# Seven block products in one more k-pair of the down projection, and wider additions for their activation sums

## The chip, the core and the metric

One core of a Trainium2 chip runs the whole program. TensorE (PE in the profile, PEld for its weight loads) multiplies, VectorE (DVE), ScalarE (ACT) and GpSimd (POOL) work beside it, and SyncE (SP) issues most of the DMAs. The metric is the device time of one launch in microseconds. Lower is better.

## The reference

One decoder layer on 256 tokens of width 2048, in float32:

```python
x = x + 0.5 * swiglu(rms_norm(x, g1), w_gate, w_up, w_down)        # FFN 1, hidden width 5632
h = rms_norm(x, gm); z = h @ w_in
x = x + concat(gated_linear_attention(z), dilated_attention(z)) @ w_out
x = x + 0.5 * swiglu(rms_norm(x, g2), w_gate2, w_up2, w_down2)     # FFN 2
# swiglu(x, g, u, d) = (silu(x @ g) * (x @ u)) @ d
```

The change is in the last product of `swiglu`, the down projection (256 x 5632 by 5632 x 2048), of both FFNs.

## The kernel before

**Splitting.** Every float32 operand is held as a rounded high part and the rest, its low part (`wh`, `wl` of weights; `hh`, `hl` and `uh`, `ul` of activations). A product is three matmuls into one PSUM bank: high by high, high by low, low by high. `split` makes the two parts: ACT copies with rounding (L113), then DVE subtracts (L114).

**The down projection.** It runs over two column pairs (`cp` 0 and 1) of 1024 output columns each, so there are four of them in the program. Each goes over the 44 blocks of 128 of the hidden width, taken two at a time as 22 k-pairs. A k-pair's weights, 256 x 1024, come by one DMA of 1 MB into a `raw` tile, of which there are three (L219, SP's queue). The order of the k-pairs of a column pair is written out by hand in `DOWN_ORDERS`: "s" for a k-pair done plainly, "g" for one done by seven products.

- A plain k-pair (`products`, L276 to L280) is two units of 128 of the hidden width; each has two token tiles, two banks and three matmuls. That makes 24 matmuls of 512 columns, and two weight splits of 1024 elements per partition on ACT and DVE.
- A k-pair by seven products (`seven_products`, L301 to L303) treats tokens, hidden and output columns as 2 x 2 blocks and needs 7 block products, so 21 matmuls. It needs sums of weight blocks: `prepare` makes four jobs of it, "plain" (a sum into the room `urs`, L240, and a split), "last" (a split of 512), "sums" (a split of the room, and two additions into `raw`, L248) and "more" (a split of what these additions left in `raw`). It also needs four sums of activation blocks, split as well: `seven_forms` makes them once for an FFN, and both column pairs use them.

The four extra accumulators of the seven products are added to the output after the last "g" of a column pair: `fold`, nine operations, one in each following step.

**What sets the order.** `weights()` prepares jobs two ahead of the unit in hand; weight tiles come from a ring of four (`WBUF`). Other work sits in the list `later`, from which a few entries are taken in each step (a unit has two steps, one for each token tile). For the down projection `later` has 32 entries: a call of `seven_forms` in every fifth, and the rest of the gate and up stage's work in the others. From this program order a planner, which runs a time line of its own, draws up the final order of each engine's queue; each queue is then worked in that order.

**Where sums are kept.** The split sums (`dforms`) live in parts of `hh` and `hl`, which the down projection does not need otherwise. `hl` 8 to 11 is the room of the "last" job. After the first column pair of FFN 1 (`renorm`, `norm_moved`) POOL moves blocks of the new activations into `hh` 8 to 15, so these parts serve no form from then on, except that those into 12 to 15 wait until form 0 has been used.

Of the kernel before, what the change touches and what calls it, by code (L numbers as in the profile page):

```python
# [14 lines left out]
F32 = mybir.dt.float32  # L15
# [3 lines left out]
ALU = mybir.AluOpType  # L19
AX = mybir.AxisListType  # L20

P = 128
S = 256
# [15 lines left out]
def _order(text):  # L39

    seven, plain = iter(range(text.count("g"))), iter(range(text.count("g"), len(text)))
    return [(next(seven), True) if c == "g" else (next(plain), False) for c in text]


FF_ORDERS = [_order("ssgssgss" if b in FF_SEVEN else "ssssssss") for b in range(FF // 512)]
DOWN_ORDERS = [_order("ssssssgssgssgsgsgsgsss"), _order("sgsssgssgssgssgsgsssss")]


def layer_kernel(tc, x, xT, gains, gla_gate_up, gla_gate_bias, gla_out_norm, att_q_norm, att_k_norm,
                 w_ff1, w_dn1, w_mix, w_low, w_out, w_ff2, w_dn2, c_sq, c_rope, c_mask, out):  # L50

    nc = tc.nc
# [3 lines left out]
    with ExitStack() as es:  # L56
# [20 lines left out]
        def t512(name):  # L77
            return cst.tile([P, 512], F32, name=name, tag="t512", bufs=4)
# [14 lines left out]
        hh = cst.tile([P, KT, S], F32R, name="hh")  # L93
# [81 lines left out]
        def jobs_of(w, orders):  # L175
            for cp, order in enumerate(orders):
                for kp, seven in order:
                    for part in ("plain", "last", "sums", "more") if seven else (0, 1):
                        yield w, cp * len(order) + kp, part

        jobs = [*jobs_of(w_ff1, FF_ORDERS), *jobs_of(w_dn1, DOWN_ORDERS)]
        jobs += [(w_mix, i, k) for i in range(3 * KT // 2) for k in range(2)] + ["low"]
        jobs += [(w_mix, i, k) for i in range(3 * KT // 2, 3 * KT) for k in range(2)]
        jobs += [(w_out, i, k) for i in range(w_out.shape[0]) for k in range(2)]
        jobs += [*jobs_of(w_ff2, FF_ORDERS), *jobs_of(w_dn2, DOWN_ORDERS)]

        AHEAD = 2
        ready = []
# [74 lines left out]
        def alt(a):  # L263

            return a.rearrange("p (b a) -> p a b", b=2)
# [24 lines left out]
        def seven_products(cs, ms, acts, forms, first, last):  # L290

            tok = [slice(t * P, (t + 1) * P) for t in range(NT)]
            a11, a12, a22 = [[a[:, acts[k][2], tok[t]] for a in acts[k][:2]] for t, k in ((0, 0), (0, 1), (1, 1))]
            s1, s3, s2, sa = [[f[:, i, :] for f in forms] for i in range(4)]

            def product(bank, a, ws, j, start, stop):  # L300
                nc.tensor.matmul(bank, lhsT=a[0], rhs=alt(ws[0][:, j, :]), start=start, stop=False)  # L301
                nc.tensor.matmul(bank, lhsT=a[0], rhs=alt(ws[1][:, j, :]), start=False, stop=False)  # L302
                nc.tensor.matmul(bank, lhsT=a[1], rhs=alt(ws[0][:, j, :]), start=False, stop=stop)  # L303

            ws = weights()
            product(ms[0], a11, ws, 0, first, last)
            product(cs[0], sa, ws, 1, False, False)
            product(cs[1], a12, weights(), 0, False, False)
            ws = weights()
            product(ms[1], s1, ws, 0, first, last)  # L310
            product(ms[3], s3, ws, 1, first, last)
            ws = weights()
            product(ms[2], s2, ws, 0, first, last)
            product(cs[3], a22, ws, 1, False, False)

        def seven_forms(acts, forms, full, sums):

            for k, (ah, al, i) in enumerate(acts):
                nc.vector.tensor_add(full[:, k * S:(k + 1) * S], ah[:, i, :].bitcast(F32), al[:, i, :].bitcast(F32))
            a11, a21, a12, a22 = [full[:, i * P:(i + 1) * P] for i in range(4)]  # L320
            sums = sums.rearrange("p (i q) -> p i q", i=4)
            nc.vector.tensor_sub(sums[:, 0, :], a22, a21)
            nc.vector.tensor_sub(sums[:, 1, :], a11, a21)
            nc.vector.scalar_tensor_tensor(sums[:, 2, :], sums[:, 0, :], -1.0, a11, op0=ALU.mult, op1=ALU.subtract)
            nc.vector.tensor_add(sums[:, 3, :], a12, sums[:, 2, :])
            split(*forms, sums)

# [81 lines left out]
        def ffn(name, done, residual, extra=None, final=False):  # L409

            with tc.tile_pool(name=name, bufs=1, reuse_waits="tile") as fp:
# [12 lines left out]
                for b in range(FF // 512):  # L424
# [23 lines left out]
                    if b == FF_SEVEN[0]:  # L448
# [8 lines left out]
                        forms = {kp: [f[:, kp] for f in fs] for kp in range(2)}  # L457
# [22 lines left out]
                dacts = [part(k) for k in range(FT)]  # L480

                def lent(a, k, i):
                    return a[:, k:k + 2, :].rearrange("p k (t q) -> p (k t) q", q=P) if i else a[:, k:k + 2, :].rearrange("p k s -> p (k s)").unsqueeze(1)

                rooms["down"] = {"sum": urs, "wh": lent(hl, 8, 0), "wl": lent(hl, 10, 0)}
                dforms = {kp + 1: [lent(hh, 2 * kp, 1), lent(hl, 2 * kp, 1)] for kp in range(4)}
                dforms[0] = [lent(hh, 12, 1), lent(hh, 14, 1)]
                dforms[5] = [lent(hl, 12, 1), lent(hl, 14, 1)]
                rest, later[:] = later[:], []
                for step in range(32):  # L490
                    kp = step // 5 - 1
                    if step % 5 == 0 and 0 <= kp < 6:
                        later.append(lambda kp=kp: seven_forms(dacts[2 * kp:2 * kp + 2], dforms[kp], t512("full"), t512("sums")))
                    else:
                        later.append(rest.pop(0) if rest else lambda: None)
                for cp in range(2):
                    def evac(t, ps, cp=cp):
                        for j in range(2):
                            c = 2 * cp + j
                            blk = xs[:, t, c * 512:(c + 1) * 512]  # L500
                            nc.vector.scalar_tensor_tensor(halves(blk), ps[j], 0.5, halves(blk), op0=ALU.mult, op1=ALU.add)
                            done(t, c, blk)

                    def fold(m, cp=cp):
                        a, b = [halves(urs[:, i, :]) for i in range(2)]
                        c = [[halves(xs[:, t, i * 512:(i + 1) * 512]) for i in (2 * cp, 2 * cp + 1)] for t in range(NT)]

                        def add(c, a, f):
                            return lambda: nc.vector.scalar_tensor_tensor(c, a, f, c, op0=ALU.mult, op1=ALU.add)
                        return [lambda: nc.scalar.activation(a, m[0], AF.Copy),  # L510
                                lambda: nc.vector.tensor_add(b, a, m[2]), add(c[0][1], a, 0.5),
                                lambda: nc.vector.tensor_add(a, b, m[3]), add(c[1][1], a, 0.5),
                                lambda: nc.vector.tensor_add(b, b, m[1]), add(c[0][0], b, -0.5),
                                lambda: nc.vector.tensor_add(a, a, m[1]), add(c[1][0], a, -0.5)]

                    holding[0] = NT - cp
                    seven_pair(dacts, DOWN_ORDERS[cp], dforms, cp, evac, fold, span=28 if cp else 32, final=final and cp == 1)
                spare.close()


# [444 lines left out]
```

## Time and profile before

| | us |
|---|---|
| median of 3 runs | 1721.78 |
| lowest and highest of them | 1718.25, 1723.28 |
| profiled execution, its own time | 1721.82 |
| its span, first to last instruction | 1720.0 |

| engine | busy us | share of the span |
|---|---|---|
| PE | 1707.9 | 99% |
| PEld | 1486.0 | 86% |
| DVE | 1399.7 | 81% |
| ACT | 936.0 | 54% |
| POOL | 506.4 | 29% |

The granted TensorE clock is 1.000 throughout. A matmul's record is longer than the distance to the next one, since matmuls are pipelined; the distance between starts is what a matmul costs. Rows of DVE overlap by about 0.08 us in the same way. The four column pairs of the down projection lie at about 455 to 565 and 565 to 677 us (FFN 1), and 1495 to 1606 and 1606 to 1716 us (FFN 2).

### The profile page before, as it was taken

To read this page: it belongs to the slowest core of one execution; us is meant where nothing else is said; L and a number is where in the kernel's file an instruction comes from. 1 tells how busy PE (TensorE), PEld (TensorE's weight loads), DVE (VectorE), ACT (ScalarE), POOL (GpSimd) and SP (SyncE) were. 2 spreads that over 40 slices of the span, in tenths; PEclk is the share of its full clock that TensorE was granted. 3 is DMA by queue.
4 is the path that set the end of the run, shared out by engine and by line. 5 is a ranking of instruction groups with operands and counts; after the bars stand their busy time and mean duration, and the time that the engine had idled before them with its cause. 6 is when DMAs were issued, how large, how long until landed. Compare 5 with 4: busy or idle time off the path is not lost.

```text
span 1720.0 us, 22310 instructions
## 1 busy us (share of the span) xinstructions
PE 1707.9 (99%) x7980; PEld 1486.0 (86%) x7980; DVE 1399.7 (81%) x1699; ACT 936.0 (54%) x1166; POOL 506.4 (29%) x1002
## 2 busy tenths in 40 slices
PE   9999999999999999999999999999999999999999
PEld 7888888888888888888888888888888888888887
DVE  6888888888899788578865667798988888898876
ACT  7555555555555555564654545555555555465453
POOL 0333333444410611054250043333333334420000
PEclk9999999999999999999999999999999999999999
DMA  8666655655675657576564466666666656665754
GB/s 344 212 228 224 216 208 213 228 211 211 239 269 220 217 208 245 185 243 231 195 205 171 149 216 236 219 221 229 228 227 227 214 208 221 222 246 215 249 205 147
DMA packets 85807, 378.62 MB, mean 220 GB/s; under 512 B 21392, under 2 KB 38800, under 8 KB 42688
## 3 DMA queue, kind: packets, MB, share of 16 engines
q1 hardware_dynamic: 50864, 350.25, 56.6%
q0 software_dynamic: 34112, 25.88, 5.3%
q8 instruction: 62, 1.02, 0.2%
q10 hardware_dynamic: 720, 1.07, 0.2%
q14 instruction: 49, 0.40, 0.1%
HBM read 354.57 MB, written 4.19 MB: 209 GB/s over the span
## 4 chain that ended last, share of the span: by engine, by line
PE 76%; DVE 11%; DMA 7%; issue 3%; ACT 2%; POOL 1%; DVEq 0%; ACTq 0%; SPq 0%; POOLq 0%
PE acc L278 18%; PE acc L280 18%; PE acc L276 18%; DVE wl L114 5%; DMA raw<-in_w_ff_dram 4%; PE tp L280 3%; PE tp L278 3%; PE tp L276 3%; PE acc L302 3%; PE acc L303 3%; PE acc L301 3%; DVE raw L248 1%; ACT wh L113 1%; DVE xs L240 1%; DMA hh<-us 1%
## 5 line engine op out<-in xcount | busy, mean ns | idle before, releaser
L113 ACT ACTIVATE wh<-raw 128x1024 fp32r<-128x1024 f32 (+1 forms) x660 | 676.0, 1047 | 476.2 <-PE acc L280 188.3
L114 DVE TENSOR_TENSOR wl<-raw,wh 128x1024 fp32r<-128x1024 f32 (+1 forms) x658 | 787.7, 1215 | 169.1 <-ACT wh L113 165.8
L135 POOL DMA_DIRECT2D xs<-us x704 | 344.4, 497 | 556.4 <-issue 353.1
L280 PE MATMUL acc<-wh,hl 128*128 128x512 f32 x1232 | 371.0, 380 | 0.0
L278 PE MATMUL acc<-wl,hh 128*128 128x512 f32 x1232 | 370.5, 380 | 0.4 <-DVE wl L114 0.3
L276 PE MATMUL acc<-wh,hh 128*128 128x512 f32 x1232 | 363.0, 381 | 2.6 <-ACT wh L113 2.6
L276 PEld LDWEIGHTS acc<-wh,hh 128*128 128x128 f32 x1232 | 232.6, 189 | 37.0 <-ACT wh L113 3.3
L278 PEld LDWEIGHTS acc<-wl,hh 128*128 128x128 f32 x1232 | 232.5, 189 | 34.5 <-DVE wl L114 1.3
L280 PEld LDWEIGHTS acc<-wh,hl 128*128 128x128 f32 x1232 | 232.6, 189 | 32.8
L278 PE MATMUL acc<-wl,uh 128*128 128x512 f32 x384 | 116.7, 379 | 0.0
L280 PE MATMUL acc<-wh,ul 128*128 128x512 f32 x384 | 116.6, 379 | 0.0
L276 PE MATMUL acc<-wh,uh 128*128 128x512 f32 x384 | 111.9, 379 | 0.2 <-ACT wh L113 0.2
L135 POOL DMA_DIRECT2D hh<-us x128 | 62.0, 499 | 124.0 <-DVE us L128 67.6
L276 PEld LDWEIGHTS acc<-wh,uh 128*128 128x128 f32 x384 | 72.5, 189 | 10.9 <-ACT wh L113 0.6
L280 PEld LDWEIGHTS acc<-wh,ul 128*128 128x128 f32 x384 | 72.6, 189 | 10.3
L278 PEld LDWEIGHTS acc<-wl,uh 128*128 128x128 f32 x384 | 72.6, 189 | 10.3
L240 DVE TENSOR_TENSOR xs<-raw 128x1024 f32<-128x1024 f32 x40 | 48.2, 1206 | 37.3 <-DMA raw<-in_w_ff_dram 37.3
L113 ACT ACTIVATE wh<-xs 128x1024 fp32r<-128x1024 f32 x40 | 42.1, 1053 | 57.3 <-DVE xs L240 42.0
L276 PE MATMUL tp<-wh,hh 128*128 128x512 f32 x240 | 73.2, 379 | 0.0
L113 ACT ACTIVATE swh<-raw 128x512 fp32r<-128x512 f32 x40 | 25.2, 630 | 88.0 <-DMA raw<-in_w_ff_dram 88.0
L278 PE MATMUL tp<-wl,hh 128*128 128x512 f32 x240 | 71.4, 379 | 0.0
L280 PE MATMUL tp<-wh,hl 128*128 128x512 f32 x240 | 71.4, 379 | 0.0
(284 smaller groups left out, 2358.9 us busy)
## 6 DMA issues: line engine op xcount, KB each, us to landing
raw<-in_w_ff_dram SPq DMA_DIRECT2D x175, 1024.0 KB, 5.1
raw<-in_w_dn_dram SPq DMA_DIRECT2D x88, 1024.0 KB, 4.9
raw<-in_w_mix_dram SPq DMA_DIRECT2D x48, 1024.0 KB, 4.9
raw<-in_w_out_dram SPq DMA_DIRECT2D x16, 1024.0 KB, 4.8
xs<-us POOLq DMA_DIRECT2D x704, 16.0 KB, 3.7
xs<-in_x_dram SPq DMA_DIRECT2D x2, 1024.0 KB, 10.6
xs<-in_x_dram POOLq DMA_DIRECT2D x2, 1024.0 KB, 5.5
hh<-us POOLq DMA_DIRECT2D x128, 16.0 KB, 3.7
```

Source lines behind the costliest of these rows:

```text
L113: nc.scalar.activation(dst_h, src, AF.Copy)
L114: nc.vector.tensor_sub(dst_l, src, dst_h.bitcast(F32))
L135: nc.gpsimd.dma_start(dst[32 * q:32 * q + 32, ..., r * n:(r + 1) * n], src[32 * r:32 * r + 32, ..., q * n:(q + 1) * n])
L240: nc.vector.tensor_add(room["sum"], b1, mid)
L248: nc.vector.tensor_add(raw[:, 1, j, :], b, raw[:, 1, j, :])
L276: nc.tensor.matmul(ps[j], lhsT=sh, rhs=alt(wh[:, j, :]), start=first and i == 0, stop=False)
L278: nc.tensor.matmul(ps[j], lhsT=sh, rhs=alt(wl[:, j, :]), start=False, stop=False)
L280: nc.tensor.matmul(ps[j], lhsT=sl, rhs=alt(wh[:, j, :]), start=False, stop=last and i == len(ws) - 1)
L301: nc.tensor.matmul(bank, lhsT=a[0], rhs=alt(ws[0][:, j, :]), start=start, stop=False)
L302: nc.tensor.matmul(bank, lhsT=a[0], rhs=alt(ws[1][:, j, :]), start=False, stop=False)
L303: nc.tensor.matmul(bank, lhsT=a[1], rhs=alt(ws[0][:, j, :]), start=False, stop=stop)
```

## The change

Three of the four column pairs get a seventh "g": both of FFN 2 (`LAST_ORDERS`) and the first of FFN 1. The second of FFN 1 keeps its six. The new sums of activations lie in `hh` 8 to 11. Seven calls of `seven_forms` now stand in every fourth entry of `later`. In `seven_forms`, two additions of 256 elements become one of 512, and two subtractions of 128 become one of 256; for this the sums s1 and s3 change places in their tile. The first "g" of a first column pair comes after five plain k-pairs instead of six.

```diff
-DOWN_ORDERS = [_order("ssssssgssgssgsgsgsgsss"), _order("sgsssgssgssgssgsgsssss")]
+DOWN_ORDERS = [_order("sssssgssgsgsgsgsgsgsss"), _order("sgsssgssgssgssgsgsssss")]
+LAST_ORDERS = [DOWN_ORDERS[0], _order("sgssgssgssgssgsgsgssss")]
...
-        jobs += [*jobs_of(w_ff2, FF_ORDERS), *jobs_of(w_dn2, DOWN_ORDERS)]
+        jobs += [*jobs_of(w_ff2, FF_ORDERS), *jobs_of(w_dn2, LAST_ORDERS)]
...
-            s1, s3, s2, sa = [[f[:, i, :] for f in forms] for i in range(4)]
+            s3, s1, s2, sa = [[f[:, i, :] for f in forms] for i in range(4)]
...
-            for k, (ah, al, i) in enumerate(acts):
-                nc.vector.tensor_add(full[:, k * S:(k + 1) * S], ah[:, i, :].bitcast(F32), al[:, i, :].bitcast(F32))
+            ah, al, i = acts[0]
+            nc.vector.tensor_add(full.rearrange("p (k s) -> p k s", k=2), ah[:, i:i + 2, :].bitcast(F32), al[:, i:i + 2, :].bitcast(F32))
             a11, a21, a12, a22 = [full[:, i * P:(i + 1) * P] for i in range(4)]
             sums = sums.rearrange("p (i q) -> p i q", i=4)
-            nc.vector.tensor_sub(sums[:, 0, :], a22, a21)
-            nc.vector.tensor_sub(sums[:, 1, :], a11, a21)
-            nc.vector.scalar_tensor_tensor(sums[:, 2, :], sums[:, 0, :], -1.0, a11, op0=ALU.mult, op1=ALU.subtract)
+            nc.vector.tensor_sub(sums[:, 0:2, :], full.rearrange("p (i q) -> p i q", i=4)[:, 0::3, :], a21.unsqueeze(1).to_broadcast([P, 2, P]))
+            nc.vector.scalar_tensor_tensor(sums[:, 2, :], sums[:, 1, :], -1.0, a11, op0=ALU.mult, op1=ALU.subtract)
             nc.vector.tensor_add(sums[:, 3, :], a12, sums[:, 2, :])
             split(*forms, sums)
...
                 dforms[5] = [lent(hl, 12, 1), lent(hl, 14, 1)]
+                dforms[6] = [lent(hh, 8, 1), lent(hh, 10, 1)]
...
-                    kp = step // 5 - 1
-                    if step % 5 == 0 and 0 <= kp < 6:
+                    kp = step // 4 - 1
+                    if step % 4 == 0 and 0 <= kp < 7:
...
-                    seven_pair(dacts, DOWN_ORDERS[cp], dforms, cp, evac, fold, span=28 if cp else 32, final=final and cp == 1)
+                    seven_pair(dacts, (LAST_ORDERS if final else DOWN_ORDERS)[cp], dforms, cp, evac, fold, span=28 if cp else 32, final=final and cp == 1)
```

## Prediction

> **What bounds the kernel now.** I read the page first, then what TensorE waited for, then the busy time of each engine in the four column pairs of the down projection, and last the time lines of one run of "g" k-pairs. The page's engine line and the waits of PE:
>
> ```profile
> PE 1707.9 (99%) x7980; PEld 1486.0 (86%) x7980; DVE 1399.7 (81%) x1699; ACT 936.0 (54%) x1166; POOL 506.4 (29%) x1002
> PE acc L276 <- ACT wh L113: 2.7, 3, 1.9
> PE tp L301 <- ACT wh L113: 1.4, 3, 0.7
> PE tp L302 <- DVE wl L114: 0.5, 1, 0.5
> ```
>
> TensorE is the bound. It hardly waits, and where it does after the start it waits for a weight split. So each matmul that goes takes its distance to the next with it, as long as the splits keep up. That distance and the time of one "g" with one "s" stand in the chain of waits (start, duration, engine and line):
>
> ```profile
> 520.89 0.86 PE acc L276 x4
> 530.60 0.86 PE acc L276 x4
> 540.31 0.86 PE acc L276 x4
> 550.02 0.86 PE acc L276 x4
> ```
>
> These are the first matmuls of the "s" between successive "g". They are 9.71 us apart, and 21 + 24 = 45 matmuls lie between, so one takes 0.2158 us. PE ran there without a pause.
>
> Do the splits keep up? Busy time in the four column pairs:
>
> ```profile
> 455.10:565.40 110.30, 110.30 (x512) 96.58 (x511) 101.66 (x137) 61.69 (x70) 16.74 (x34) 1.00 0.64 234
> 565.40:676.60 111.20, 110.58 (x511) 96.18 (x510) 88.80 (x97) 59.37 (x70) 35.36 (x72) 1.00 0.66 226
> 1495.30:1605.70 110.40, 110.40 (x513) 96.50 (x512) 101.42 (x137) 60.86 (x68) 16.74 (x34) 1.00 0.64 234
> 1605.70:1715.90 110.20, 110.20 (x511) 96.19 (x509) 81.71 (x84) 52.52 (x53) 0.00 (x0) 1.00 0.55 195
> ```
>
> The columns are the stretch and its length, then PE, PEld, DVE, ACT, POOL, clock, DMA share and rate. In the two first column pairs DVE is busy 92% of the time, since the forms of an FFN are made there; in the last it has 28 us to spare.
>
> **The change part by part.**
>
> *Matmuls.* Three k-pairs go from 24 to 21: 9 x 0.2158 = 1.94 us less on PE, all of it on the path. The Trainium skill, TensorE: Matmul & The Clock Gate, section "Back-to-back issue gap", gives about 131 ns for one matmul of 512 columns in a sustained stream. By that the gain would be an estimated 1.18 us and the sum 0.76 us higher; the rows above show 0.2158, so the rule doesn't hold here.
>
> *Sums of activations.* Distances between DVE starts, in FFN 2:
>
> ```profile
> 1526.53 0.28 DVE L322 TENSOR_TENSOR sums<-full 128x128 f32<-128x128 f32 x1
> 1526.73 0.28 DVE L323 TENSOR_TENSOR sums<-full 128x128 f32<-128x128 f32 x1
> 1526.94 0.68 DVE L114 TENSOR_TENSOR hl<-sums,hh 128x512 fp32r<-128x512 f32 x1
> 1527.54 0.28 DVE L324 SCALAR_TENSOR_TENSOR sums<-sums,full 128x128 f32<-128x128 f32 x1
> 1527.74 0.75 DVE L319 TENSOR_TENSOR full<-uh,ul 128x256 f32<-128x256 f32 x2
> 1528.41 1.21 DVE L114 TENSOR_TENSOR wl<-raw,wh 128x1024 fp32r<-128x1024 f32 x1
> 1529.55 0.28 DVE L325 TENSOR_TENSOR sums<-full,sums 128x128 f32<-128x128 f32 x1
> ```
>
> An operation of 128 elements takes 0.20 us, of 256 0.33 (two of them 0.67), of 512 0.60, of 1024 1.14. Two of 256 as one of 512 save 0.07, two of 128 as one of 256 another 0.07. A call falls from 2.07 to 1.93 us of DVE, and the 16 calls there are save 2.2 us. Those in the gate and up stages (4) I take at nothing: they are 0.56 us spread over two stages. Their bounds are 0 and -0.56.
>
> *The added "g" on DVE.* A "g" needs 1.14 (sum) + 1.14 + 0.60 + 1.14 + 1.14 (four splits) + 2 x 0.60 = 6.36 us, an "s" 2 x 1.14 = 2.28. In a first column pair DVE gets 4.08 + 1.93 (form 6) - 6 x 0.14 = 5.2 us more: 101.7 becomes 106.9, of the 109.6 that PE then needs. In the last one 81.7 becomes 85.8. ACT gets three splits of 1024, one of 512 and a form's split for two of 1024, about 2.4 us on 62 of 110: covered. The DMAs stay as they are, one `raw` of 1 MB for a k-pair, and neither POOL nor SP gets another instruction.
>
> *The last column pair of FFN 2.* The gain there is whole. The last "g" comes one k-pair (5.2 us) later, and `fold` with it. In the trace DVE's additions of the fold are past before these rows, and DVE idles until the last outputs:
>
> ```profile
> 1706.69 1.22 DVE L114 TENSOR_TENSOR wl<-raw,wh 128x1024 fp32r<-128x1024 f32 x1 [1.36 <-ACT wh L113]
> 1712.51 1.29 DVE L501 SCALAR_TENSOR_TENSOR xs<-acc,xs 128x512 f32<-128x512 f32 x2 [4.59 <-PE acc L280]
> ```
>
> The split before it too has 1.36 us of idle time ahead of it. A unit takes PE 12 x 0.2158 = 2.59 us, and one split and two additions of 512 take DVE 1.14 + 2 x 0.60 = 2.34, so the fold keeps pace over the last four k-pairs. Cost 0; the 4.59 us are the cover that would have to go first.
>
> *What moves in the queues.* In `later` the load of `xs` (L478, POOL) comes one entry later, after form 2 now. In FFN 1 it was issued at 499.55 and first used by the fold at 548.51, so one entry costs nothing; the cover is 49 us:
>
> ```profile
> 499.55 0.54 POOL L478 DMA_DIRECT2D xs<-in_x_dram  x1 [19.71 <-DVE ul L114]
> 548.51 0.68 DVE L509 SCALAR_TENSOR_TENSOR xs<-urs,xs 128x512 f32<-128x512 f32 x1
> ```
>
> POOL's moves into `hh` 8 to 11 begin in FFN 1 after the first column pair's outputs, three "s" after form 6 was last read: no new wait.
>
> *The first column pairs.* Here the price is open. Two things happen. First, the run of alternating "g" and "s" grows: before, "g" stand at places 9, 12, 14, 16, 18 (counted from 0) and three times a "g" follows two places on; now at 8, 10, 12, 14, 16, 18, five times. What such a run costs DVE, in FFN 1 and then FFN 2 (`urs<-raw` is a "g"'s first sum, and the first of three merged L114 behind it is the "more" split of the "g" before):
>
> ```profile
> 515.59 1.23 DVE L240 TENSOR_TENSOR urs<-raw 128x1024 f32<-128x1024 f32 x1 [0.67 <-DMA raw<-in_w_dn_dram]
> 526.64 1.23 DVE L240 TENSOR_TENSOR urs<-raw 128x1024 f32<-128x1024 f32 x1 [2.07 <-DMA raw<-in_w_dn_dram]
> 527.78 3.49 DVE L114 TENSOR_TENSOR wl<-raw,wh 128x1024 fp32r<-128x1024 f32 x3
> 536.19 1.23 DVE L240 TENSOR_TENSOR urs<-raw 128x1024 f32<-128x1024 f32 x1 [0.72 <-DMA raw<-in_w_dn_dram]
> ...
> 1556.06 1.23 DVE L240 TENSOR_TENSOR urs<-raw 128x1024 f32<-128x1024 f32 x1 [1.10 <-DMA raw<-in_w_dn_dram]
> 1566.74 1.22 DVE L240 TENSOR_TENSOR urs<-raw 128x1024 f32<-128x1024 f32 x1 [1.84 <-DMA raw<-in_w_dn_dram]
> 1577.05 1.23 DVE L240 TENSOR_TENSOR urs<-raw 128x1024 f32<-128x1024 f32 x1 [1.48 <-DMA raw<-in_w_dn_dram]
> 1578.19 3.49 DVE L114 TENSOR_TENSOR wl<-raw,wh 128x1024 fp32r<-128x1024 f32 x3
> ```
>
> The next "g"'s sum stands ahead of this "g"'s "more" split in DVE's queue, and it waits for its DMA. The DMA goes out only when the "s" between has been split, since there are three `raw` tiles, and right behind another:
>
> ```profile
> 517.97 0.33 SPq L219 DMA_DIRECT2D raw<-in_w_dn_dram  x1
> 520.24 0.33 SPq L219 DMA_DIRECT2D raw<-in_w_dn_dram  x1
> ```
>
> From 520.24 to the sum at 526.64 are 6.4 us; the sum, "more" and the two splits of the next "s" then take 1.14 + 3.49 before the next DMA of that kind can go. So the loop turns in 11.05, 9.55, 10.68 and 10.31 us (distances of the sums), against PE's 9.71. It eats up the lead of the splits. In FFN 2 the lead is gone at the end of the run: the "more" split that starts at 1578.19 ends some 0.06 us before its first matmul, which has to wait 0.10 us (0.32 to the next instead of 0.22):
>
> ```profile
> 1579.47 0.48 PE L302 MATMUL tp<-wl,hh 128*128 128x512 f32 x1
> 1579.79 0.38 PE L303 MATMUL tp<-wh,hl 128*128 128x512 f32 x1
> ```
>
> The longer run has four loops with a "g"'s sum ahead; the fifth is the run's end, where no "g" follows and "more" isn't held up. I take the first as the first ones were (11.05 and 10.68, so 1.16 over PE's 9.71) and three as the second ones (9.55 and 10.31, 0.22 over): 1.82 us. The lead on entry, at the second "g", is:
>
> ```profile
> 503.52 2.36 DVE L114 TENSOR_TENSOR wl<-raw,wh 128x1024 fp32r<-128x1024 f32 x2 [1.20 <-ACT wh L113]
> 505.62 0.38 PE L302 MATMUL tp<-wl,hh 128*128 128x512 f32 x1
> ...
> 1543.53 2.36 DVE L114 TENSOR_TENSOR wl<-raw,wh 128x1024 fp32r<-128x1024 f32 x2 [1.20 <-ACT wh L113]
> 1545.79 0.38 PE L302 MATMUL tp<-wl,hh 128*128 128x512 f32 x1
> ```
>
> The first of the two merged splits ends some 1.22 us after its start, 0.88 and 1.04 us ahead of PE, 0.96 in the mean. That leaves 1.82 - 0.96 = 0.9 us of waiting for a column pair. Bounds: 0 (all loops at 9.55) and 4 x 1.34 - 0.96 = 4.4 (all at 11.05).
>
> Second, the first "g" comes one "s" earlier: 24 x 0.2158 = 5.18 us less of PE's time, 2.28 + 0.84 = 3.1 us less of DVE's work to that point, so the lead at the second "g" falls by 2.1, from 0.96 to -1.1. But four of the six forms that stand ahead of it in the program serve only later "g", and their 4 x 1.93 = 7.7 us can move into the loop's waits of 0.7 to 2.1 us. Bounds 0 and 1.2 (0.88 - 2.06); I take 0.3, nearer the end at which the forms yield, since their small operations already stand between the splits in the rows of 1526 to 1529.
>
> *Sum.* 1721.82 (the profiled time, within 0.04 of the median) - 1.94 - 0.10 (the wait at 1579.47, contained in the new 0.9) + 2 x (0.9 + 0.3) = 1722.2 us.
>
> **Rivals.** *All of it is hidden.* DVE has 110.3 - 101.7 = 8.6 us idle in the first column pairs, more than the 5.2 us to be added; if forms and splits fill the waits, no matmul waits longer: 1721.82 - 1.94 - 0.10 = 1719.8. Against it: part of that idle time is waiting for DMAs behind which a queue worked in order stands still.
>
> *The run of "g" is DMA bound (slower).* If each loop takes as long as the longest shown, 11.05 us, and the forms don't yield, a first column pair loses 4.4 + 1.2 = 5.6 us: 1721.82 - 2.04 + 11.2 = 1731.0. It decides above 7.2 us of waits in both together, 3.6 each, (3.6 + 0.96) / 4 = 1.14 over PE's pace, so from a loop of 10.85 us on. For it: two of four loops are at or near that. Against it: the second loops of both runs were shorter. The Trainium skill, DMA: Bandwidth & Descriptors, section "Bandwidth", gives 6.15 us for a DMA of 1 MB. By that a loop would be an estimated 6.15 + 4.6 = 10.8 us, and the time about 1727; the page's row of the profile has a lower median, with single cases near the rule's:
>
> ```profile
> raw<-in_w_dn_dram SPq DMA_DIRECT2D x88, 1024.0 KB, 4.9
> ```
>
> *The planner arranges other stages anew.* The waits of PE listed first (4.6 us together) could shrink to nothing or double with any edit: 1721.82 - 4.6 = 1717 to 1726.
>
> **How the numbers follow.** About 0.3% (5.2 us) is what a measurement of this kernel can tell from no change. Chances: the forecast, partly eaten up, 0.52 (its own range 1720.5 to 1725); all hidden 0.27; DMA bound 0.16; other stages 0.05. The range 1718.5 to 1727.5 reaches from somewhat under the all-hidden case to the middle of the DMA-bound one. Slower by over 0.3% (above 1727.0) takes most of the DMA-bound case and some of the last, 0.13; faster (below 1716.6) needs more than all gains named, 0.04; the rest, 0.83, is within.
>
> **What would show it.** PE with 9 matmuls fewer, at the same distance. Waits of PE for "more" splits at the "g" of places 8 to 16 of both first column pairs, 1.2 us in each; sums `urs<-raw` there 9.6 to 11 us apart, each ended by its DMA. No wait in the last column pair, and DVE's idle time before the last outputs still over 1 us. L319 at 128x512, about 0.68 us each, 18 of them. The prediction is wrong if PE shows no new wait (forms filled the gaps), if it waits at the first "g" already for several microseconds, or if the difference lies in the gate and up or attention stages.

## The result and the profile after

The changed kernel takes 1734.0 us, median of 6 runs (1730.77 to 1737.02), against 1720.55 of before (6 runs): 1.0075 times the time, 95% interval 1.0062 to 1.0088. It is slower by 13 us; 1722.2 was forecast, with a range of 1718.5 to 1727.5. The profiled execution took 1737.02 us itself, the longest of its six runs, with a span of 1735.2.

The page's engine line, and then what PE waited for in the first three column pairs, in order, leaving out waits of up to 0.2 us each (us in total, times, longest):

```profile
PE 1713.1 (99%) x7971; PEld 1483.4 (85%) x7971; DVE 1414.5 (82%) x1692; ACT 938.7 (54%) x1174; POOL 507.8 (29%) x1002
```

```profile
PE tp L303 <- DVE wl L115: 2.1, 3, 1.2
PE tp L302 <- ACT wh L114: 1.4, 1, 1.4
...
PE acc L303 <- DVE wl L115: 1.5, 1, 1.5
PE acc L302 <- ACT wh L114: 0.5, 1, 0.5
...
PE tp L303 <- DVE wl L115: 1.9, 3, 1.2
PE tp L302 <- ACT wh L114: 1.4, 1, 1.4
```

In the fourth pair PE waits for nothing. (Lines of the code are one higher than before.) The two first column pairs with the busy time of each engine, columns as in the prediction:

```profile
456.50:573.30 116.80, 112.66 (x510) 94.96 (x509) 106.04 (x134) 61.96 (x71) 16.77 (x34) 1.00 0.61 218
1505.60:1621.80 116.20, 112.38 (x510) 95.08 (x509) 106.75 (x134) 61.68 (x72) 16.78 (x34) 1.00 0.61 220
```

A first column pair now has 7 x 21 + 15 x 24 = 507 matmuls, 109.4 us at 0.2157; it takes 116.8 and 116.2. So nine matmuls went, as the engine line says, and 7 us of pauses came into each first pair.

To place them, the distance between each matmul of 512 columns and the next was taken wherever it is over 0.235 us, and 0.2157 taken off. These pauses of PE, in us, with the median time of 4 to 12 runs and its ratio to runs of before on the same chip (whose medians were 1720.48 to 1721.9). In those with an asterisk some matmuls behind a pause ran at half pace, 0.427 us each, as the last section shows; they make 0.8 to 1.7 us of the number, in `x4_pool` up to 3:

| kernel | FFN 1, pair 1 | FFN 1, pair 2 | FFN 2, pair 1 | FFN 2, pair 2 | us | ratio, 95% |
|---|---|---|---|---|---|---|
| before | 0.0 | 1.2 | 0.1 | 0.0 | 1720.55 | 1 |
| after | 7.2 | 3.1 | 6.5 | 0.0 | 1734.0 | 1.0075, 1.0062 to 1.0088 |
| x1_wide | 0.2 | 1.7 | 0.0 | 0.0 | 1724.47 | 1.0013, 1.0003 to 1.0023 |
| x2_last | 0.0 | 4.6* | 0.6 | 0.0 | 1724.06 | 1.0017, 1.0007 to 1.0028 |
| x12_lastnarrow | 0.1 | 1.5 | 3.5 | 0.0 | 1721.7 | 0.9995, 0.9985 to 1.0006 |
| x10_narrow7 | 8.0* | 1.6 | 6.7 | 0.0 | 1734.3 | 1.0068, 1.0052 to 1.0084 |
| x18_oneloop | 0.4 | 2.2 | 1.6 | 0.0 | 1725.03 | 1.0020, 1.0009 to 1.0032 |
| x15_shift | 2.4 | 2.9 | 1.9 | 0.0 | 1726.41 | 1.0030, 1.0019 to 1.0040 |
| x11_sixearly | 5.0 | 4.7* | 4.2 | 0.0 | 1731.66 | 1.0053, 1.0038 to 1.0068 |
| x8_sixfirst | 6.8* | 5.6* | 7.0* | 0.0 | 1734.82 | 1.0068, 1.0054 to 1.0082 |
| x16_breaklate | 6.2* | 4.9* | 5.6 | 0.0 | 1733.64 | 1.0074, 1.0057 to 1.0090 |
| x3_pinforms | 7.6* | 2.9 | 6.4* | 0.0 | 1730.66 | 1.0048, 1.0034 to 1.0062 |
| x5_pinsum | 6.1* | 2.2 | 6.1* | 0.0 | 1731.66 | 1.0056, 1.0042 to 1.0069 |
| x6_pinboth | 11.2* | 2.2 | 11.2* | 0.0 | 1740.53 | 1.0116, 1.0103 to 1.0130 |
| x7_before_pinsum | 1.2 | 2.2 | 1.1 | 0.0 | 1722.76 | 1.0013, 1.0004 to 1.0022 |
| x9_oneform | 1.5 | 6.6* | 3.9 | 0.0 | 1731.3 | 1.0062, 1.0048 to 1.0075 |
| x4_pool | 17.1* | 15.2* | 17.3* | 0.0 | 1763.77 | 1.0251, 1.0237 to 1.0265 |

The pauses are those of one profiled execution each, the times medians. How far one execution can stand off another is seen in `x1_wide` and `x2_last`: up to 1534 us their order on DVE is the same, and FFN 1's second pair still has 1.7 us of pauses in the one and 4.6 in the other. From before to after the two spans differ by 15.2 us: -1.9 for the matmuls, +7.2, +2.0 and +6.4 for the first three pairs, and +1.5 in the first 22 us of the program, which the change doesn't touch; the gate and up and attention stages differ by under 0.5 each.

**What a first pair's pauses are.** DVE around the second "g" (place 8) of FFN 1, and PE there:

```profile
498.36 0.68 DVE L249 TENSOR_TENSOR raw<-urs,raw 128x512 f32<-128x512 f32 x1
498.96 0.41 DVE L323 TENSOR_TENSOR sums<-full 128x256 f32<-128x256 f32 x1
499.30 0.68 DVE L320 TENSOR_TENSOR full<-uh,ul 128x512 f32<-128x512 f32 x1
499.90 0.68 DVE L115 TENSOR_TENSOR hl<-sums,hh 128x512 fp32r<-128x512 f32 x1
500.50 0.68 DVE L115 TENSOR_TENSOR ul<-xs,uh 128x512 fp32r<-128x512 f32 x1
501.11 0.68 DVE L249 TENSOR_TENSOR raw<-raw 128x512 f32<-128x512 f32 x1
...
501.16 0.38 PE L304 MATMUL tp<-wh,hl 128*128 128x512 f32 x1
502.93 0.48 PE L302 MATMUL tp<-wh,hh 128*128 128x512 f32 x1 [1.39 <-ACT wh L114]
```

Between the two additions that "more" needs, the planner (the "scheduler" of the expectations) has put a subtraction, an addition and a split of forms, and a split of the FFN's tail: 2.15 us. The three forms are those of the sixth, seventh and fifth "g", which PE begins at 543, 553 and 532 us only. ACT can round the "more" blocks only after the second addition, and PE stands 1.56 us at 501.16 and 3.1 us in all around place 8. DVE has no free moment then; the windows show it (DVE's is the third busy time, behind PE's and PEld's):

```profile
475.00:490.00 15.00, 14.89 (x68) 12.40 (x68) 14.90 (x22) 9.18 (x12) 4.48 (x9) 1.00 0.66 239
490.00:505.00 15.00, 13.15 (x59) 10.55 (x57) 15.00 (x23) 7.89 (x11) 0.54 (x1) 1.00 0.60 211
505.00:520.00 15.00, 14.50 (x64) 11.80 (x65) 14.96 (x19) 8.38 (x10) 0.00 (x0) 1.00 0.64 236
520.00:535.00 15.00, 14.53 (x68) 12.41 (x67) 10.38 (x12) 7.59 (x8) 0.00 (x0) 1.00 0.56 209
```

DVE is full for 45 us and then has 4.6 us idle in the next 15. From place 14 on DVE stands idle for the DMA of each "g"'s sum, as the prediction said. Here are the sums of places 5, 10, 12, 14, 16 and 18, and behind those of 10 to 16 the row that begins with the "more" split of the "g" before:

```profile
474.91 1.23 DVE L241 TENSOR_TENSOR urs<-raw 128x1024 f32<-128x1024 f32 x1 [1.35 <-DMA raw<-in_w_dn_dram]
...
501.71 1.21 DVE L241 TENSOR_TENSOR urs<-raw 128x1024 f32<-128x1024 f32 x1
503.98 1.21 DVE L115 TENSOR_TENSOR wl<-raw,wh 128x1024 fp32r<-128x1024 f32 x1
512.79 1.22 DVE L241 TENSOR_TENSOR urs<-raw 128x1024 f32<-128x1024 f32 x1
514.53 4.62 DVE L115 TENSOR_TENSOR wl<-raw,wh 128x1024 fp32r<-128x1024 f32 x4
524.01 1.23 DVE L241 TENSOR_TENSOR urs<-raw 128x1024 f32<-128x1024 f32 x1 [2.40 <-DMA raw<-in_w_dn_dram]
525.15 2.35 DVE L115 TENSOR_TENSOR wl<-raw,wh 128x1024 fp32r<-128x1024 f32 x2
535.17 1.23 DVE L241 TENSOR_TENSOR urs<-raw 128x1024 f32<-128x1024 f32 x1 [2.32 <-DMA raw<-in_w_dn_dram]
536.31 2.35 DVE L115 TENSOR_TENSOR wl<-raw,wh 128x1024 fp32r<-128x1024 f32 x2
545.24 1.23 DVE L241 TENSOR_TENSOR urs<-raw 128x1024 f32<-128x1024 f32 x1 [1.25 <-DMA raw<-in_w_dn_dram]
```

From sum to sum the loops turn in 11.08, 11.22, 11.16 and 10.07 us; the first is no wait for a DMA, since DVE works through it without a pause. What PE needs is "more", and from "more" to "more" the turns are 10.55, 10.62, 11.16 and 10.07 (to 546.38), together 3.6 us over four of PE's 9.71. PE's pauses behind place 8 are 3.6 us too (FFN 2: 3.3 and 3.4): nothing of the loops is hidden any more.

### The profile page after: what moved, and what is told of

The parts are those of the page before. It is cut to its first block, busy times and chain, and to the rows that moved or that the text cites. A ratio compares the mean times of both kernels' runs of the same rounds, so it can differ in the third digit from the quotient of the medians.

```text
span 1735.2 us, 22294 instructions
## 1 busy us (share of the span) xinstructions
PE 1713.1 (99%) x7971; PEld 1483.4 (85%) x7971; DVE 1414.5 (82%) x1692; ACT 938.7 (54%) x1174; POOL 507.8 (29%) x1002
## 4 chain that ended last, share of the span: by engine, by line
PE 72%; DVE 14%; DMA 7%; issue 3%; ACT 2%; POOL 1%; DVEq 0%; ACTq 0%; SPq 0%
PE acc L279 16%; PE acc L281 16%; PE acc L277 16%; DVE wl L115 7%; PE tp L277 4%; PE tp L281 4%; PE tp L279 4%; PE acc L303 3%; PE acc L304 3%; DMA raw<-in_w_ff_dram 3%; PE acc L302 3%; DMA raw<-in_w_dn_dram 2%; DMA xs<-us 2%; ACT wh L114 1%; DVE raw L249 1%
## 5 line engine op out<-in xcount | busy, mean ns | idle before, releaser
L279 PE MATMUL acc<-wl,uh 128*128 128x512 f32 x364 | 111.5, 381 | 0.1
L281 PE MATMUL acc<-wh,ul 128*128 128x512 f32 x364 | 110.9, 379 | 0.0
L277 PE MATMUL acc<-wh,uh 128*128 128x512 f32 x364 | 106.7, 381 | 1.3 <-ACT wh L114 1.2
L277 PEld LDWEIGHTS acc<-wh,uh 128*128 128x128 f32 x364 | 68.2, 189 | 13.3 <-ACT wh L114 3.9
L279 PEld LDWEIGHTS acc<-wl,uh 128*128 128x128 f32 x364 | 68.1, 189 | 11.7 <-DVE wl L115 2.3
L281 PEld LDWEIGHTS acc<-wh,ul 128*128 128x128 f32 x364 | 68.8, 189 | 9.8
```

The lines of the kernel that those rows point to most:

```text
L277: nc.tensor.matmul(ps[j], lhsT=sh, rhs=alt(wh[:, j, :]), start=first and i == 0, stop=False)
L279: nc.tensor.matmul(ps[j], lhsT=sh, rhs=alt(wl[:, j, :]), start=False, stop=False)
L281: nc.tensor.matmul(ps[j], lhsT=sl, rhs=alt(wh[:, j, :]), start=False, stop=last and i == len(ws) - 1)
```

## The experiments

Theory A: PE comes to the second "g" before DVE has done what stands ahead of its "more" split. Theory B: the loops with a "g"'s sum ahead are slower than PE, each by its own excess. Rivals: C, the wider operations let the planner set another order elsewhere; D, DVE is simply full.

**Wide operations alone, and the last pair alone.** `x1_wide` is before with the new `seven_forms`; `x2_last` adds `LAST_ORDERS` for FFN 2's second pair; `x12_lastnarrow` is that with the old `seven_forms`; `x10_narrow7` is after with the old `seven_forms`.

```diff
-                    if step % 5 == 0 and 0 <= kp < 6:          # x2_last, x12_lastnarrow, against before
+                    if final and step == 31:
+                        kp = 6
+                    if (step % 5 == 0 and 0 <= kp < 6) or kp == 6:
```

> The kernel before with only the wider operations of seven_forms; every column pair keeps its six 'g'. Theory A (backlog: too much of DVE's work stands ahead of the first 'more' splits of the longer run) and theory B (loop: in an alternating run the next 'g''s sum waits for its DMA ahead of 'more') both say that the 13 us come from the seventh 'g' alone: 1720.6 us, at most 0.5 less, and no wait at the 'g' of the first column pairs. Rival C (the wider operations let the scheduler set another order, which holds up splits elsewhere, as in FFN 1's second column pair, 2 us more after): several microseconds slower, 1723 to 1730.

> The kernel before with the wider operations, and the seventh 'g' in FFN 2's second column pair alone. A and B: that pair has no alternating run and DVE has 28 us idle there, so three matmuls go at no cost: 0.65 us below the kernel with the wider operations alone, about 1719.9 us, PE without waits in that pair. C: like the wider operations alone or slower, 1723 to 1730.

> The kernel before with one change: the seventh 'g' in FFN 2's second column pair, with the operations of seven_forms as before and the seventh form made at the end of the list. Three matmuls less on PE with DVE 28 us idle there: 0.65 us below before, 1719.9; no waits in that pair. The added form of 2.1 us in FFN 2's first column pair could cost up to as much: 1722. If the list's other order moves FFN 1's stages: up to 1724.

> The kernel after with the narrower operations of before in seven_forms, all else as after: DVE gets 0.14 us more for each form. If the seventh 'g' makes the loss, 1734 to 1736 us. If the wider operations make part of it by the order that the scheduler sets (rival C; alone they came out at 1.0013 of before), up to 2 us less, 1731 to 1733.

The wide operations alone put no pause into the first pairs: the seventh "g" and its order make the loss there. By time, `x1_wide` is slower than before by 0.13%, some 2 us, where A and B had expected none, so C has a part. `x2_last` against `x12_lastnarrow`, another pair with wide and narrow operations, differs by 0.22%; after against `x10_narrow7` by 0.07%, less than their intervals, though the latter's first pair has 1.4 us at half pace. So the size of this part isn't settled. The seventh "g" in the last pair costs nothing in that pair, in any kernel that has it. The 0.65 us that it saves are less than the runs can tell; `x2_last` and `x12_lastnarrow` came out above the 1719.9 expected. The 3.5 us of `x12_lastnarrow` in FFN 2's first pair are mostly one pause of 2.7, for a "more" behind a sum that waited 3.64 us for a DMA which took 7.7 us to land.

What C is in FFN 1's second pair can be seen. First after, then `x10_narrow7`: DVE, and SP's issue of the next "g"'s weights:

```profile
631.72 2.35 DVE L115 TENSOR_TENSOR wl<-raw,wh 128x1024 fp32r<-128x1024 f32 x2
...
636.77 1.23 DVE L241 TENSOR_TENSOR urs<-raw 128x1024 f32<-128x1024 f32 x1 [2.70 <-DMA raw<-in_w_dn_dram]
637.92 1.22 DVE L115 TENSOR_TENSOR wl<-raw,wh 128x1024 fp32r<-128x1024 f32 x1
...
640.90 0.33 SPq L220 DMA_DIRECT2D raw<-in_w_dn_dram  x1
...
646.82 1.23 DVE L241 TENSOR_TENSOR urs<-raw 128x1024 f32<-128x1024 f32 x1 [2.23 <-DMA raw<-in_w_dn_dram]
```

```profile
631.62 3.49 DVE L115 TENSOR_TENSOR wl<-raw,wh 128x1024 fp32r<-128x1024 f32 x3
...
636.60 1.23 DVE L241 TENSOR_TENSOR urs<-raw 128x1024 f32<-128x1024 f32 x1 [1.49 <-DMA raw<-in_w_dn_dram]
...
638.99 0.33 SPq L220 DMA_DIRECT2D raw<-in_w_dn_dram  x1
...
644.95 1.23 DVE L241 TENSOR_TENSOR urs<-raw 128x1024 f32<-128x1024 f32 x1 [1.06 <-DMA raw<-in_w_dn_dram]
```

With the narrow operations three splits are done before the sum waits, with the wide ones two; the third then stands behind the wait, and "last" with it. The next `raw` tile comes free 1.7 us later after the sum (its DMA is issued after 4.13 instead of 2.39 us), and the next "g" turns in 10.05 instead of 8.35 us. At place 14 PE then waits 1.49 us for a split in the one and 0.20 in the other. The other kernels bear this out. The three with narrow operations (before, `x12_lastnarrow`, `x10_narrow7`) have the same order on DVE there and pause 0.5 to 1.1 us at place 14. The nine with wide ones that keep all forms and pin no sum have another, the same in all nine, and pause 1.2 to 2.8 us: 1.5 more in the mean.

**The order of the "g", with six of them.** These three are after with `LAST_ORDERS = DOWN_ORDERS`, six forms (`0 <= kp < 6`) and another first order. They do as many matmuls as before.

```diff
-DOWN_ORDERS = [_order("ssssssgssgssgsgsgsgsss"),     # before, and x1_wide
+DOWN_ORDERS = [_order("sssssgssgssgsgsgsgssss"),     # x15_shift
+DOWN_ORDERS = [_order("ssssssgssgsgsgsgsgssss"),     # x18_oneloop
+DOWN_ORDERS = [_order("sssssgssgsgsgsgsgsssss"),     # x11_sixearly
```

> The wider operations with six 'g' in every column pair, but the first column pairs in the order of the kernel after without its last 'g': 'sssssgssgsgsgsgsgsssss', and the forms as early as after. No matmul goes against before. A: the backlog at the second 'g' is nearly that of after (one form of 1.9 us less, which came last): 2 to 3 us in each. B: four 'g' follow two places on instead of three, one loop more, 0.6 to 1.3 us. Both: 1726 to 1731. If the seventh 'g' itself (its 4 us of splits) makes the loss: about 1721 to 1724.

> Six 'g' in each pair, wider operations, no matmul less than before; the first column pairs' order of before with all 'g' one place earlier: 'sssssgssgssgsgsgsgssss' (places 5, 8, 11, 13, 15, 17), so as many close followers as before (three). A (less time for DVE's work ahead of the second 'g's 'more'): some 2 us of waits at place 8 of each, as with 'sssssgssgsgsgsgsgsssss', and little behind it: 1725 to 1727. B (the count of loops with a 'g''s sum ahead): as the wider operations alone, 1721 to 1724.

> The same with the order 'ssssssgssgsgsgsgsgssss' (places 6, 9, 11, 13, 15, 17): the first two 'g' where they were before, but four close followers instead of three. A: no wait at place 9, as the wider operations alone, 1721 to 1724. B: one loop more, with the lead of about 1 us used up: 1 to 2 us of waits at places 13 to 17 in each: 1724 to 1727.

The two causes can be told apart here. The first "g" one place earlier, with as many close followers, costs 2.2 us in the one first pair and 1.9 in the other (A). In FFN 1, 1.7 of the 2.4 us of pauses lie at place 8 and 0.7 around the first "g". What PE waited for there in `x15_shift`, the "more" splits of place 8:

```profile
PE tp L302 <- ACT wh L114: 0.9, 1, 0.9
```

One loop more with the first "g" where they were costs 0.2 and 1.6 us (B). Both together cost 4.8 and 4.2, more than the sums of 2.4 and 3.5. The turns from "more" to "more" say why. In `x18_oneloop` the three from place 9 on exceed PE's 9.71 us by 1.3 and 2.6 us in all, and PE pauses 0.4 and 1.6: the splits come into the run with a lead that pays 0.9. In `x11_sixearly` those from place 8 on exceed it by 2.4 and 1.9, and PE pauses 2.5 and 2.0 behind that place: the lead was used up at place 8, and each loop's excess falls on PE whole. The turns themselves vary with the landing of single DMAs, 9.7 to 11.6 us in these two kernels, so how much more than the sum it is isn't settled. By the medians 9 of the 13 us come without any seventh "g"; some of the 9 may belong to FFN 1's second pair, which has 4.7 us of pauses in `x11_sixearly` and 1.7 in `x1_wide` with the same order on DVE.

D falls by the same kernels; here are the first pair of FFN 1 in `x18_oneloop` and in `x11_sixearly`, with the same work on DVE (101.3 and 101.2 us), some 0.4 us less than before, and 0.4 and 5.0 us of pauses:

```profile
455.90:566.60 110.70, 110.63 (x512) 96.31 (x511) 101.28 (x125) 60.65 (x70) 16.82 (x34) 1.00 0.63 231
```

```profile
454.40:569.70 115.30, 112.28 (x513) 95.70 (x512) 101.16 (x125) 60.57 (x70) 16.80 (x34) 1.00 0.61 224
```

**Seven "g" in other orders.**

```diff
-DOWN_ORDERS = [_order("sssssgssgsgsgsgsgsgsss"),     # after
+DOWN_ORDERS = [_order("ssssssgsgsgsgsgsgsgsss"),     # x8_sixfirst
+DOWN_ORDERS = [_order("sssssgsgsgssgsgsgsgsss"),     # x16_breaklate
```

> The kernel after with the first column pairs' order 'ssssssgsgsgsgsgsgsgsss': the first 'g' comes after six 's', as before, and all seven alternate. A (backlog): one 's' more ahead of the first 'g' gives DVE 5.2 us of PE's time for 2.3 us of splits, so some 2 to 3 us of the waits at the second 'g' go in each first column pair: 1728 to 1730 us. B (loops): there is one loop more with a 'g''s sum ahead, so that 1.3 us come back in each: 1731 to 1733. If only the loops counted it would be 1734 or more.

> The kernel after with seven 'g' in every pair it had them, but the two successive 's' in the run put later: 'sssssgsgsgssgsgsgsgsss' (places 5, 7, 9, 12, 14, 16, 18). A: the second 'g' comes one place earlier still, with all the forms ahead of it: 2 to 3 us more waiting at places 7 and 9 in each than after, partly given back by the pause at 10 and 11: 1734 to 1738. B: the same number of loops, split three and two, and the lead made up between: 1730 to 1733.

Neither helps. In `x8_sixfirst` the second "g" is at place 8 as it was, since only one "s" is left between the first two. PE pauses 4.8 and 4.3 us around it, 1.0 and 1.2 of them at half pace, against 3.1 after in both. So the place of the second "g" counts more than that of the first, which A as written had missed. In `x16_breaklate` it is at 7, with 5.1 (1.2 at half pace) and 3.8 us around it; the later run is shorter, and the sum is nearly the same. Seven "g" in 22 places, with five "s" ahead and three behind, leave room for one pair of successive "s" only.

**The order on DVE.** The planner sets the order of an engine's operations by its own estimates, and where the forms stand in the list has little to say: with a form in every fourth entry (`x18_oneloop`) and in every fifth (`x1_wide`), the orders on DVE and ACT are the same until behind the splits of all six forms, at 505 us, where the k-pairs begin to differ. So here operations were bound to their place in the program; `x6_pinboth` has both edits.

```diff
# x3_pinforms: forms at steps 4, 10, 16, 22, 28, 33, 38 of a list of 44
-            nc.vector.tensor_add(full.rearrange("p (k s) -> p k s", k=2), ah[:, i:i + 2, :].bitcast(F32), al[:, i:i + 2, :].bitcast(F32))
+            tc.keep_in_program_order(nc.vector.tensor_add(full.rearrange("p (k s) -> p k s", k=2), ah[:, i:i + 2, :].bitcast(F32), al[:, i:i + 2, :].bitcast(F32)))
# x5_pinsum, x7_before_pinsum: the down projection's sum and both halves of "last"
-                nc.vector.tensor_add(room["sum"], b1, mid)
+                ins = nc.vector.tensor_add(room["sum"], b1, mid)
+                if room is rooms.get("down"):
+                    tc.keep_in_program_order(ins)
...
+                    tc.keep_in_program_order(nc.scalar.activation(wh[:, 0, :], raw[:, 1, 1, :], AF.Copy))
+                    tc.keep_in_program_order(nc.vector.tensor_sub(wl[:, 0, :], raw[:, 1, 1, :], wh[:, 0, :].bitcast(F32)))
```

> The kernel after, with the seven forms spread over 44 steps and the first addition of each kept in its place in the program's order, so that they can't be made early. A: the wait of 3.1 us at the second 'g' (place 8) of each first column pair goes to under 1 us, and with it some 5 us in all: about 1729 us. B: the lead gained is lost again in the loops of 11.1 us that follow, waits only move to places 10 to 16: 1732 to 1735.

> The kernel after, with the down projection's weight sum and the split 'last' kept in the program's order, so that 'more' and the splits of the 's' between no longer stand behind the wait for the next 'g''s DMA. B: the loops of the alternating run fall from 11.1 us to PE's 9.7, the waits at places 8 to 16 go, 6 us for each first column pair: 1720 to 1723 us. A: the waits at place 8 (3.1 us in each) stay, the later ones go: about 1727 us. Neither: if 'last' and the sum in their places make DVE wait elsewhere, 1734 or more.

> The kernel before with the weight sum and 'last' pinned in the program's order. B: the few waits there (1.2 us in FFN 1's second column pair, 0.1 in FFN 2's first) go, or their place is taken by a wait for 'last' behind the forms as in the pinned kernel after: 1719.5 to 1722. D has no word on it. If the pinned order by itself costs 4 us at the first 'g', as the pinned kernel after shows at its places 5 and 6, it is 1725 or more here too.

> The kernel after with both edits: the forms spread over 44 steps with the first addition of each pinned, and the weight sum and 'last' pinned, so that neither stands ahead of 'more'. Each edit alone gained 2.3 to 3.3 us and left 6 us of waits in each first column pair, at other places: forms late leaves the loops (places 8 to 12), the pinned sum leaves the backlog at the first 'g'. A and B together: waits in each first column pair under 2 us, 1722 to 1725 us. Rival D (DVE, with 106.9 of 109.6 us of work, is simply full, and any order only moves the waits): 5 us or more of waits stay in each, 1729 or more.

With the forms late, the pause at place 8 of FFN 1 falls to 0.25 us and comes back at 10, 12 and 14 as 1.0, 1.8 and 4.2 us (1.7 at half pace): B takes what A gives, as B expected of the waits; the time, 1730.7, lies between the two expected. With the sum pinned, the loops turn in 9.6 to 10.0 us and no sum waits for its DMA, as B expected, and the pauses from place 10 on shrink to 1.0 and 1.4 us. But 5.0 and 4.7 us (1.7 and 1.1 at half pace) come at the first "g", whose "last" now stands behind three forms: A takes what B gives. `x7_before_pinsum` pays for the same pin at the first "g" of the first three pairs, 1.1, 2.1 and 1.1 us, and is rid of the wait at place 14; at 1722.76 it lies between the two times expected. Both edits together were expected to be the cure and are the worst order. As A and B were written for it, neither foresaw this. D's time for it came true, but DVE isn't full there: it is busy 106.0 of 120.7 us. DVE in a loop of `x6_pinboth`:

```profile
505.71 1.22 DVE L241 TENSOR_TENSOR urs<-raw 128x1024 f32<-128x1024 f32 x1
...
512.08 0.69 DVE L115 TENSOR_TENSOR hl<-sums,hh 128x512 fp32r<-128x512 f32 x1 [0.70 <-ACT hh L114]
...
515.30 3.50 DVE L115 TENSOR_TENSOR wl<-raw,wh 128x1024 fp32r<-128x1024 f32 x3 [1.20 <-ACT wh L114]
518.72 1.22 DVE L241 TENSOR_TENSOR urs<-raw 128x1024 f32<-128x1024 f32 x1
```

A form stands in program order between a "g"'s sum and its "last", and with its first addition pinned the rest of its chain comes into the loop. DVE stands idle 0.70 us for ACT's rounding of the form and 1.20 us for that of "more". Two loops turn in 13.0 us so, the one with the last form in 11.5, and the one without a form in 10.0.

**Less work on DVE.** `x9_oneform` makes form 0 alone and multiplies by it in every "g"; `x4_pool` moves the weight sum.

```diff
+                dforms = {kp: dforms[0] for kp in range(7)}                    # x9_oneform
-                    if step % 4 == 0 and 0 <= kp < 7:
+                    if step == 4:
-                nc.vector.tensor_add(room["sum"], b1, mid)                      # x4_pool
+                (nc.gpsimd if room is rooms.get("down") else nc.vector).tensor_add(room["sum"], b1, mid)
```

> The kernel after, but only the first form is made in each FFN and every 'g' multiplies by it: six of seven calls of seven_forms and their splits are left out, some 15 us of DVE in each first column pair. A: with no backlog the waits at place 8 go, and the lead on entry (over 3 us) covers most of the loops: 1.5 us or less of waits in each, 1721 to 1724. B: the loops still turn in 11 us, four or five of them, so 4 x 1.3 less a lead of 3 leaves 2 us or more at places 12 to 16: 1724 to 1727. D: DVE has 18 us idle, no waits: 1719 to 1721.

> The kernel after with the down projection's weight sums on GpSimd: DVE loses 1.14 us for each 'g' and nothing of DVE's waits for a 'g''s DMA any more. B: the loop of DMA, sum and splits opens, 'more' comes early, waits under 3 us in each first column pair: 1721 to 1727, if GpSimd needs less than some 8 us for a sum of 1024 elements that has 9.7 us of time. A: the waits at place 8 stay at 2 to 3 us each: 1726 to 1729. Against both: GpSimd needs longer or holds up DVE's operations while it runs, 1735 or more.

Without six of seven forms the first pairs' pauses fall from 7.2 to 1.5 and from 6.5 to 3.9 us, while DVE has 15 and 18 us idle in them:

```profile
455.90:567.00 111.10, 109.95 (x509) 95.82 (x508) 95.66 (x105) 59.86 (x67) 16.76 (x34) 1.00 0.63 230
1500.30:1613.80 113.50, 110.99 (x510) 95.47 (x509) 95.70 (x104) 58.13 (x65) 16.77 (x34) 1.00 0.62 226
```

So idle time of DVE doesn't prevent pauses (D). At place 8 nothing is left in FFN 1 and 0.9 us in FFN 2; the rest is at places 7 to 14, in FFN 1 all at place 14 behind a loop of 11.1 us (B for the most part). The median misses all three expectations, since FFN 1's second pair has 6.6 us: PE waited 3.5 us there for POOL's moves of activations (`hh<-us`), and 1.5 went at half pace. Why the moves came later is not shown.

`x4_pool` misses A and B by far and is the "against both" of its expectation. GpSimd's sum takes 2.65 us in the mean and stands behind its DMA issues, and all forms came ahead of the first "g"'s additions; PE stood 9.4 us at that place. GpSimd's sum also holds up an operation of VectorE:

```profile
480.87 2.73 DVE L325 TENSOR_TENSOR sums<-full,sums 128x128 f32<-128x128 f32 x1
...
481.08 2.36 POOL L241 TENSOR_TENSOR urs<-raw 128x1024 f32<-128x1024 f32 x1
```

The addition of 128 elements, of a kind that takes 0.28 us elsewhere, ended only 0.16 us after GpSimd's sum. It is so at each of the 27 sums of this trace: a VectorE operation that began during one ended 0.16, 0.28, 0.55 or 1.08 us behind it, by its 128, 256, 512 or 1024 elements, as if it had run only then.

No kernel beat the one before. A fourth `raw` tile, which would let the next "g"'s DMA go earlier, was not tried.

## Why the prediction was wrong

- *Nine matmuls, 1.94 us:* right; 7971 are left at the same distance. The Trainium skill's 131 ns (TensorE: Matmul & The Clock Gate, section "Back-to-back issue gap") is not seen after either.
- *The last column pair costs nothing:* right. PE waits for nothing there, and DVE's cover of 4.59 us before the last outputs is as it was:

```profile
1727.71 1.29 DVE L502 SCALAR_TENSOR_TENSOR xs<-acc,xs 128x512 f32<-128x512 f32 x2 [4.59 <-PE acc L281]
```

- *Fewer DVE operations:* right in size (0.68 us at 128x512), but they brought another order, and FFN 1's second pair has 2.0 us more pauses, some 1.5 of it by that order as the twelve kernels at place 14 show. The prediction asked only what the operations cost and had no term for that pair; the rival of other stages allowed 4.6 us either way.
- *The first "g" one "s" earlier, 0.3 us:* this step failed first. Its bound of 1.2 us at the second "g" assumed the splits' lead to fall by 2.1 us; and 0.3 was taken on the belief that forms which serve later "g" yield. They don't: all seven were made by 512 us, while DVE idled from 520 on. Nor was 1.2 a bound: it left out that the earlier sum would come ahead of its own DMA. In FFN 1 DVE stood idle for it at place 5, 1.35 us after (the row at 474.91) and 1.42 in `x15_shift`; before, the first "g"'s sum, at 476.61, waited for nothing. Around place 8 PE paused 3.1 us in each first pair, ten times the term. `x15_shift` shows this step alone at 1.9 to 2.2 us.
- *The run of loops, 0.9 us:* the mechanism was right and the size was off. The loops were taken as 1 x 10.87 and 3 x 9.93, 1.82 us over PE's pace; from "more" to "more" they were 10.55, 10.62, 11.16 and 10.07 in FFN 1, 3.6 over. The short loop of before, 526.64 to 536.19, was no second kind. Its DMA went out at 531.29, 4.65 us after the sum, and from there to the next sum were 4.90:

```profile
531.29 0.33 SPq L219 DMA_DIRECT2D raw<-in_w_dn_dram  x1
```

After, "last" of the next "g" stands ahead of the second split (the first of the two at 528.03); the DMA goes out 5.26 us after the sum, and to the next sum, at 535.17, are 5.90:

```profile
527.42 0.68 DVE L115 TENSOR_TENSOR hl<-raw,hl 128x512 fp32r<-128x512 f32 x1
528.03 2.35 DVE L115 TENSOR_TENSOR wl<-raw,wh 128x1024 fp32r<-128x1024 f32 x2
...
529.27 0.33 SPq L220 DMA_DIRECT2D raw<-in_w_dn_dram  x1
```

So 0.6 us of the 1.6 between the two loops is DVE's order and 1.0 the landing of one DMA. In the trace of before a 1 MB DMA that goes out 2 to 3 us behind another lands after 5.9 us in the median of 72, with 4.8 and 8.3 at the ends, and one alone after 4.9. The 4.90 of the short loop was a quick one, and the prediction took it for a property of the loop.

- *The lead of 0.96 us to pay for them:* gone before the run began, as the step before had failed. The two steps were added up as if independent; `x11_sixearly`, where nothing of the loops is paid, against `x18_oneloop`, where 0.9 us is, shows that they aren't.
- *The rivals.* The slower rival, "DMA bound and the forms don't yield", was what happened in kind: the forms don't yield, and of the four loops three in FFN 1 and two in FFN 2 are over its 10.85 us. Its 5.6 us a pair were 7.2 and 6.4, and its 1731.0 us lay 3 below the median. That it came so near is luck in part: it gave 4.4 us to the loops and 1.2 to the lost lead, and PE paused 3.4 and 3.1 us from place 10 on, 3.8 and 3.4 up to place 9. It had a chance of 0.16. The row against it, the shorter second loops, misled.

## What to carry to other kernels

A bound engine that never waits can still hang by a lead of 1 us: work out the lead of each producer at the places that the edit moves, and treat what uses it up and what then needs it as one term. Work that "can be done later" isn't, unless something makes the planner put it later; look in the trace whether it did so before. And where a queue worked in order waits for a DMA whose buffer is freed by work behind that wait, count the loop with all that may stand in it and with the usual landing of its DMA, not with the shortest turn seen.

## What the runs showed of the hardware

PE can fall to half its clock after a pause. In `x2_last`, FFN 1's second pair, by the windows' clock and the wait of PE ahead of it:

```profile
640.00:644.00 4.00, 4.00 (x11) 3.22 (x12) 4.00 (x5) 2.10 (x3) 0.00 (x0) 0.57 0.74 268
```

```profile
639.93 0.48 PE L303 MATMUL acc<-wl,hh 128*128 128x512 f32 x1 [2.25 <-DVE wl L115]
```

After a wait of 2.25 us eight matmuls followed one another at 0.427 us instead of 0.2157, 1.7 us more. The fall doesn't always come. In `x10_narrow7` PE pauses 3.1 us at place 8 in both first pairs, by the same steps, the longest 1.83 us; behind them the clock falls in FFN 1 and not in FFN 2:

```profile
504.00:507.50 3.50, 3.50 (x9) 2.84 (x10) 3.50 (x6) 2.25 (x4) 0.00 (x0) 0.52 0.82 293
1550.90:1554.40 3.50, 3.50 (x15) 2.77 (x16) 3.50 (x6) 2.52 (x4) 0.00 (x0) 1.00 0.85 290
```

So a pause of about 2 us may cost nearly twice its length, and its length alone doesn't say when. The Trainium skill, TensorE: Matmul & The Clock Gate, section "What's actually happening", gives half rate after an idle window of about 3.4 us, and has that window run free of the kernel's start. That the fall doesn't always come would agree with a free-running window, but no run here shows the window itself. By that length most of the pauses here would be too short, and the measurement decides: but for `x4_pool` and `x9_oneform`, with pauses of 3.6 us and more, the fall came behind pauses whose longest step was 1.4 to 2.7 us, with shorter ones close by. In the profiled execution of after none is seen in the down projection.
